# Layer 1's running means as products with banded matrices on TensorE, and router logits and expert rows summed in PSUM

## The chip, the cores and the metric

The kernel runs on one core of one Trainium2 chip. The metric is the device time of one execution in microseconds (us), the median of several runs. Beside it stands one profiled execution, with its own time and with a trace of every engine: TensorE (PE, with its weight loads as PEld), VectorE (DVE), ScalarE (ACT), GpSimd (POOL), and SyncE (SP), which issues most DMAs.

## The reference, cut to what matters

The program runs three blocks in a row on 256 tokens of width 1024 (and 16 meta tokens ahead of them in the first block). The change concerns the first block's layer 1: a pool of running means over the last 2, 4, 8 and 16 tokens for four groups of 256 columns, and the router of the experts behind it.

```python
def multiscale_pool(h, w_group, scale):
    hg = h.reshape(B, L, N_POOL_GROUPS, POOL_GROUP).astype(jnp.float32)
    pos = jnp.arange(L)
    for gi, w in enumerate(POOL_WINDOWS):            # (2, 4, 8, 16)
        xg = hg[:, :, gi, :]
        cs = jnp.cumsum(xg, axis=1)
        cs_shift = jnp.pad(cs, ((0, 0), (w, 0), (0, 0)))[:, :L]
        count = jnp.minimum(pos + 1, w).astype(jnp.float32)[None, :, None]
        outs.append((cs - cs_shift) / count - xg)
    pooled = jnp.stack(outs, axis=2).astype(h.dtype)
    mixed = jnp.einsum("blgc,gcd->blgd", pooled, w_group)
    return mixed.reshape(B, L, D_MODEL) * scale

def moe_swiglu(h, w_router, e_gate, e_up, e_down):
    logits = (h @ w_router).astype(jnp.float32)
    top_vals, top_idx = lax.top_k(logits, TOP_K)     # 2 of 8 experts
...
# layer 0: h += conformer_conv(rms_norm(h));  h += swiglu(rms_norm(h))
# layer 1: h += multiscale_pool(rms_norm(h)); h += moe_swiglu(rms_norm(h))
```

## The kernel before

**Stages.** Layer 0 (conformer convolution and a dense feed-forward), the pool and the router of layer 1, the experts of layer 1, then the second and the third block. All engines work from one program; each engine takes its instructions in a fixed order, and semaphores order them between engines. Weights stream from HBM in tiles of up to 1 MB; each is split by ACT (`whi`, L143) and DVE (`wlo`, L144) into a high and a low half, and each product of weights becomes three (`mm3`, L149 to L151).

**End of layer 0.** In `first_dense` the feed-forward's down projection runs over t = 0 to 3, two column tiles of 128 columns each. A t is 132 products of 128x272 into `pd` (22 tiles of the hidden width, three products, two column tiles). Then DVE adds `pd` to the residual `xT`, which lies column by token (L466), ACT squares it, ACT and DVE split it with the norm's gain (`xh`, `xl`), and 12 products with the pool's group weights (`pwh`, `pwl`) give two tiles of `mixed`, which ACT scales on its way out of PSUM (L480). The products of a t stand in PE's order among the first `pd` products of the next t; those of t = 3 stand behind the last `pd` product.

**Pool.** The group product is linear, so it stands ahead of the running means, and 1/rms (`r`) is needed only behind it. After t = 3, PE sums the squares (`ss`, L223), ACT and DVE form `r` (L227, L228), DVE and POOL multiply `mixed` by it (`z`, L647), POOL subtracts `z` from `xT` (L650), and DVE forms the running sums by scans along the tokens (L656, L659) and adds them to `xT` (L662). PE has 34 products without use in its order meanwhile (`K.heat`, L243, `HEAT1`).

**Router.** PE forms the logits experts by tokens (L700), and turns `xT` into rows token by column (L705), which ACT copies out twice (`xhi`, `row`) and from which POOL forms `xlo` (L708). The logits are turned (`LT`, L716 and L719), and `choose` takes the two best experts of each token by a chain of small DVE operations, up to the one-hot sum `M` (L755). PE forms slot numbers and counts from `M` (L757 to L764), with eight more idle products ahead of them (`HEAT2`), and DVE sorts the experts by load (`order`, L785).

**Experts.** PE gathers the rows of each expert by products with a selection matrix (L841), ACT and DVE split them (`gh`, `gl`), and the experts' products follow. SP loads the first 12 expert tiles ahead of the router's result; further tiles wait on SP for `order`, and for the buffers.

Of the kernel before, what the change touches and what calls it, by code (L numbers as in the profile page):

```python
# [8 lines left out]
F32 = mybir.dt.float32  # L9
# [22 lines left out]
HEAT0, HEAT1, HEAT2 = 10, 34, 8  # L32


def f(x):
    return x.bitcast(F32)
# [321 lines left out]
def first_dense(K, I, xT, r1, mixed):  # L358

# [6 lines left out]
    with ExitStack() as s0:  # L366
# [44 lines left out]
        with tc.tile_pool(name="ffn0", bufs=1, reuse_waits="tile") as fp:  # L411
# [39 lines left out]
            ss = K.tp_tile([P, T0], name="ss3")  # L451
            pw = [K.raw_tile([P, KC, 256], name=f"pw{n}", dt=F32R) for n in "hl"]
            K.split(*pw, K.load(I["pool_w_group"][0].rearrange("g (k p) n -> p (g k) n", p=P)))
            for t in range(4):
# [9 lines left out]
                for j in range(2):  # L464
                    c = 2 * t + j
                    nc.vector.tensor_add(xT[:, c, :], pd[j], xT[:, c, :])  # L466
                    K.add_square(fp, ss, xT[:, c, :], c, acc=acc)
                    if c == 0:
                        K.warm(AF.Sqrt, xT[:, c, :], square=True)
                xh, xl = (fp.tile([P, 2, T0], F32R, name=f"x{n}", bufs=2) for n in "hl")  # L470
                for j in range(2):
                    K.gain_split(xh[:, j, :], xl[:, j, :], xT[:, 2 * t + j, :], "mix1", 2 * t + j)
                for j in range(2):
# [6 lines left out]
                    nc.scalar.activation(mixed[:, c, :], ps, AF.Copy, scale=K.v("pool_scale", c))  # L480
            K.rstd(fp, r1, ss)
# [155 lines left out]
def first_pool(K, xT, mixed, r):  # L637

    tc, nc = K.tc, K.nc
    with tc.tile_pool(name="pool", bufs=1, reuse_waits="tile") as pp:
        z = pp.tile([P, KC, NMETA + T0], F32, name="z")
        nc.gpsimd.memset(z[:, :, 0:NMETA], 0.0)
        for g in (0, 1, 3, 2):
            cs = slice(2 * g, 2 * g + 2)
            (nc.gpsimd if g == 3 else nc.vector).tensor_mul(z[:, cs, NMETA:], mixed[:, cs, :],  # L647
                                                            r[:, None, :].to_broadcast([P, 2, T0]))
            if g:
                nc.gpsimd.tensor_sub(xT[:, cs, NMETA:], xT[:, cs, NMETA:], z[:, cs, 2 * NMETA:])  # L650
        for g in range(4):
            cs, w = slice(2 * g, 2 * g + 2), 2 << g
            win = pp.tile([P, 2, T0], F32, name="win", bufs=2)
            if g == 0:

                nc.vector.tensor_sub(win, z[:, cs, NMETA - 1:NMETA + T0 - 1], z[:, cs, NMETA:])  # L656
            else:
                for j in range(2):
                    nc.vector.tensor_tensor_scan(win[:, j, :], z[:, 2 * g + j, NMETA:],  # L659
                                                 z[:, 2 * g + j, NMETA - w:NMETA + T0 - w], 0.0,  # L660
                                                 op0=OP.add, op1=OP.subtract)
            nc.vector.scalar_tensor_tensor(xT[:, cs, NMETA:], win[:, :, NMETA:], 1.0 / w, xT[:, cs, NMETA:],  # L662
                                           op0=OP.mult, op1=OP.add)
# [5 lines left out]
class Moe:  # L669


    def __init__(self, K, I, pool, h3T, row, wr, i8, slots):
# [20 lines left out]
        with ExitStack() as s:  # L693
            tmp = s.enter_context(tc.tile_pool(name="route", bufs=1, reuse_waits="tile"))
            K.heat(K.onesr[:, None, :].to_broadcast([P, 4, P]), HEAT1)
            pl = K.mm_tile([NE, SEQ])

            def logits(c0, c1):
                for c in range(c0, c1):
                    nc.tensor.matmul(pl, wr[:, c, :], h3T[:, c, :], start=c == 0, stop=c == KC - 1)  # L700

            def turned(h, i, ps):
                ns = slice(h * 512, (h + 1) * 512)
                for q in range(4):
                    nc.tensor.transpose(ps[:, q * P:(q + 1) * P], h3T[:, 4 * h + q, i * P:(i + 1) * P], K.ident)  # L705
                nc.scalar.copy(self.xhi[:, i, ns], ps)
                nc.scalar.copy(row[:, i, ns], ps)
                nc.gpsimd.tensor_sub(self.xlo[:, i, ns], row[:, i, ns], f(self.xhi[:, i, ns]))  # L708

            logits(0, 4)  # L710
            turned(0, 0, K.tp_tile([P, 512]))
            logits(4, 6)
            turned(0, 1, K.tp_tile([P, 512]))
            logits(6, 8)
            LT = tmp.tile([NE, SEQ], F32, name="LT")
            nc.vector.tensor_copy(LT, pl)  # L716
            L = K.mm_tile([P, 2, NE])
            for i in range(2):
                nc.tensor.transpose(L[:, i, :], LT[:, i * P:(i + 1) * P], K.ident[0:NE, 0:NE])  # L719
            for i in range(2):  # L720
                turned(1, i, K.acc_tile([P, 512]))
            K.heat(self.xhi[:, 1, 0:512], HEAT2)
            self.choose(tmp, L, i8)
# [6 lines left out]
    def choose(self, tmp, L, i8):  # L730
# [31 lines left out]
        pc = K.tp_tile([P, NE])  # L762
# [283 lines left out]
def router_weights(K, I, pool):  # L1046

    nc = K.nc
    wr = pool.tile([P, KC, NE], F32, name="wr")
# [3 lines left out]
    i8 = pool.tile([P, 2, NE], F32, name="i8")  # L1053
# [5 lines left out]
def first_moe(K, I, h3T, row, router, routed, ahead, cap=P):  # L1059
    tc, nc = K.tc, K.nc  # L1060
    with ExitStack() as s0:
        pool = s0.enter_context(tc.tile_pool(name="moe", bufs=1, reuse_waits="tile"))
        K.more, K.bufs["more"] = s0.enter_context(tc.tile_pool(name="more", bufs=1, reuse_waits="tile")), 2
        moe = Moe(K, I, pool, h3T, row, *router, K.slots)
# [775 lines left out]
def body(tc, I, out):  # L1840
    nc = tc.nc
    with ExitStack() as ctx:
# [4 lines left out]
        r1 = cp.tile([P, T0], F32, name="r1")  # L1847
        mixed = cp.tile([P, KC, T0], F32, name="mixed")
        first_dense(K, I, xT, r1, mixed)
        cp = cols.enter_context(tc.tile_pool(name="cols2", bufs=1, side="right", reuse_waits="tile"))  # L1850
        router = router_weights(K, I, cp)
        first_pool(K, xT, mixed, r1)
# [44 lines left out]
```

## Time and profile before

| | |
|---|---|
| median of 3 runs | 2075.14 us (2074.33 to 2076.29) |
| profiled execution, own time | 2078.04 us |
| its span, first to last instruction | 2076.3 us (1.74 us of the time lie around it) |
| mean granted TensorE clock | 0.979 |
| PE busy | 1969.0 us, 95% of the span |
| DVE, ACT, POOL busy | 1598.0, 1252.4, 45.6 us |
| HBM read, mean rate | 502.39 MB, 243 GB/s |

The times of the trace are counted from the span's start. The last `pd` product of layer 0 begins at 370.82 us, and the first gather of expert rows at 401.03 us.

### The profile page before, as it was taken

What the parts mean: (1) busy time and instruction counts of PE and PEld (TensorE: products, weight loads), DVE (VectorE), ACT (ScalarE), POOL (GpSimd) and SP (SyncE); (2) the same over time, 40 slices, a digit from 0 to 9 for tenths busy, and PEclk for the clock granted to TensorE, in tenths of its full rate; (3) what the DMA queues carried; (4) which work ended last, traced back from release to release, by engine and by line L of the source; (5) the groups of instructions that cost most, each with busy time, mean ns of one, the idle gap of its engine ahead of it and who ended that gap; (6) DMA issues with size and microseconds to landing.
All of it is one profiled execution on the core that took longest, in us unless ns stands there. A gap on an engine that the chain in (4) does not pass through costs nothing. (4 is left out here: it accounts for less than half of the span.)

```text
span 2076.3 us, 29433 instructions
## 1 busy us (share of the span) xinstructions
PE 1969.0 (95%) x11342; PEld 1690.3 (81%) x11342; DVE 1598.0 (77%) x1949; ACT 1252.4 (60%) x1479; POOL 45.6 (2%) x74
## 2 busy tenths in 40 slices
PE   8999999899898998889988999998999999999998
PEld 7989999678676876668766778777889978989997
DVE  6967665788898988888888888887667677676664
ACT  6555444467786777766777677675356455645443
POOL 1100000200000000000000000001000010000000
PEclk8999999999999999999999999999999999999999
DMA  7115564589998999989999899985334553545552
GB/s 229 62 42 184 182 206 160 204 314 359 343 403 307 355 363 345 388 290 363 353 338 390 300 347 361 347 305 139 105 106 135 183 158 120 171 164 174 184 187 77
DMA packets 236269, 505.44 MB, mean 243 GB/s; under 512 B 12058, under 2 KB 130974, under 8 KB 236120
## 3 DMA queue, kind: packets, MB, share of 16 engines
q1 hardware_dynamic: 229268, 499.36, 68.6%
q10 hardware_dynamic: 5652, 2.35, 0.6%
q0 software_dynamic: 1200, 1.77, 0.3%
q8 instruction: 91, 1.49, 0.3%
q14 instruction: 58, 0.48, 0.1%
HBM read 502.39 MB, written 1.05 MB: 242 GB/s over the span
## 5 line engine op out<-in xcount | busy, mean ns | idle before, releaser
L144 DVE TENSOR_TENSOR wlo<-raw,whi 128x2048 fp32r<-128x2048 f32 (+3 forms) x618 | 1084.4, 1776 | 203.5 <-issue 72.6
L143 ACT CAST whi<-raw 128x2048 fp32r<-128x2048 f32 (+3 forms) x618 | 913.0, 1497 | 407.0 <-PE mm L150 138.7
L149 PE MATMUL mm<-uhi,whi 128*128 128x256 f32 (+2 forms) x1152 | 331.0, 290 | 4.5 <-ACT whi L143 2.5
L150 PE MATMUL mm<-ulo,whi 128*128 128x256 f32 (+2 forms) x1152 | 331.1, 288 | 0.0
L151 PE MATMUL mm<-uhi,wlo 128*128 128x256 f32 (+2 forms) x1152 | 330.0, 287 | 0.4 <-DVE wlo L138 0.4
L150 PE MATMUL mm<-wlo,gh 128*128 128x512 f32 x560 | 223.6, 399 | 5.4 <-DVE wlo L144 5.3
L149 PEld LDWEIGHTS mm<-uhi,whi 128*128 128x128 f32 (+1 forms) x1152 | 220.4, 193 | 8.9 <-ACT uhi L249 3.1
L149 PE MATMUL mm<-whi,gh 128*128 128x512 f32 x560 | 215.0, 402 | 9.6 <-ACT whi L143 6.8
L151 PEld LDWEIGHTS mm<-uhi,wlo 128*128 128x128 f32 (+1 forms) x1152 | 220.5, 192 | 2.8 <-issue 1.0
L151 PE MATMUL mm<-whi,gl 128*128 128x512 f32 x560 | 222.5, 397 | 0.0
L150 PEld LDWEIGHTS mm<-ulo,whi 128*128 128x128 f32 (+1 forms) x1152 | 221.1, 192 | 1.3 <-issue 0.7
L910 PE MATMUL mm<-wlo,gh 128*128 128x512 f32 x336 | 129.8, 421 | 34.9 <-DVE wlo L144 33.6
L149 PEld LDWEIGHTS mm<-whi,gh 128*128 128x128 f32 x560 | 106.1, 190 | 34.9 <-ACT whi L143 7.2
L150 PEld LDWEIGHTS mm<-wlo,gh 128*128 128x128 f32 x560 | 105.8, 189 | 34.8 <-DVE wlo L144 10.1
L909 PE MATMUL mm<-whi,gh 128*128 128x512 f32 x336 | 123.1, 402 | 2.7 <-ACT whi L143 2.7
L151 PEld LDWEIGHTS mm<-whi,gl 128*128 128x128 f32 x560 | 105.7, 189 | 24.5
L910 PEld LDWEIGHTS mm<-wlo,gh 128*128 128x128 f32 x336 | 59.5, 191 | 67.6 <-DVE wlo L144 58.2
L150 PE MATMUL py<-wlo,mhh 128*128 128x512 f32 x280 | 112.3, 401 | 0.0
L151 PE MATMUL py<-whi,mhl 128*128 128x512 f32 x280 | 110.8, 396 | 0.0
L150 PE MATMUL mm<-vlo,whi 128*128 128x272 f32 x352 | 102.4, 291 | 0.0
L151 PE MATMUL mm<-vhi,wlo 128*128 128x272 f32 x352 | 101.7, 289 | 0.0
L149 PE MATMUL py<-whi,mhh 128*128 128x512 f32 x280 | 101.6, 396 | 0.0
(646 smaller groups left out, 3159.6 us busy)
## 6 DMA issues: line engine op xcount, KB each, us to landing
raw<-in_moe_w_gate_dram SPq DMA_DIRECT2D x112, 1024.0 KB, 7.0
raw<-in_moe_w_up_dram SPq DMA_DIRECT2D x112, 1024.0 KB, 6.7
raw<-in_moe_w_down_dram SPq DMA_DIRECT2D x112, 1024.0 KB, 7.1
raw<-in_w_in_dram SPq DMA_DIRECT2D x40, 1024.0 KB, 5.2
raw<-in_w_ffn_in_dram SPq DMA_DIRECT2D x22, 1024.0 KB, 5.1
raw<-in_conv_w_pw_dram SPq DMA_DIRECT2D x12, 1024.0 KB, 10.2
raw<-in_ffn_w_gate_dram SPq DMA_DIRECT2D x11, 1024.0 KB, 5.4
raw<-in_ffn_w_up_dram SPq DMA_DIRECT2D x11, 1024.0 KB, 5.4
```

The costliest lines, as they stand in the source:

```text
L143: nc.scalar.copy(hi[:, ks, :], raw[:, ks, :])
L144: nc.vector.tensor_sub(lo[:, ks, :], raw[:, ks, :], f(hi[:, ks, :]))
L149: mm(out, lhi, rhi, start=start, stop=False)
L150: mm(out, lhi, rlo, start=False, stop=False)
L151: mm(out, llo, rhi, start=False, stop=stop)
L909: nc.tensor.matmul(out, hi, whi, start=start, stop=False)
L910: nc.tensor.matmul(out, hi, wlo, start=False, stop=stop)
```

## The change

A class `Mix` takes the place of `first_pool`. It needs no scan: with tokens on the partitions, a running mean over w tokens is a product with a banded 128x128 matrix, `diag` (1/w within the band, and -1 on the diagonal), plus a small product with `over` for the tokens ahead of the 128. The matrices are built by DVE from an iota (`start`), and their rows are scaled by 1/rms of each token (`factors`), so that `mixed` itself is not multiplied.

- Each tile of `mixed` is turned as it arrives (`turn`): three transposes and three small products with the router's weights, into one PSUM tile `mixt`, from which DVE and ACT copy rows (`mixr`) and partial logits (`mixl`).
- The sum of squares is formed token by token in one column (`sst`, six products of one column).
- The rows that the experts need are summed in four PSUM tiles `row`: `xT` turned by products with the identity (`own_rows`), the banded products (`window_rows`), and a product with zeros that closes the sum (`close`). Logits are summed token by expert in `L`, in the same way.
- ACT forms `xhi` and `row` from PSUM, DVE forms `xlo` from PSUM; POOL's part is gone. `HEAT1` is gone, `HEAT2` is 16 in place of 8.

```diff
-HEAT0, HEAT1, HEAT2 = 10, 34, 8
+HEAT0, HEAT2 = 10, 16
...
                 for j in range(2):
                     c = 2 * t + j
                     nc.vector.tensor_add(xT[:, c, :], pd[j], xT[:, c, :])
-                    K.add_square(fp, ss, xT[:, c, :], c, acc=acc)
+                    sq = acc if c == 0 else fp.tile([P, T0], F32, tag="sq", name="sq", bufs=2)
+                    nc.scalar.activation(sq, xT[:, c, :], AF.Square)
+                    if 0 < c < KC - 1:
+                        nc.vector.tensor_add(acc, acc, sq)
...
+                if t == 3:
+                    mix.factors(acc, sq)
...
-                    nc.scalar.activation(mixed[:, c, :], ps, AF.Copy, scale=K.v("pool_scale", c))
-            K.rstd(fp, r1, ss)
+                    mixed = fp.tile([P, T0], F32, name="mixed", bufs=2)
+                    nc.scalar.activation(mixed, ps, AF.Copy, scale=K.v("pool_scale", c))
+                    mix.turn(c, mixed)
...
-def first_pool(K, xT, mixed, r):
...
-        for g in (0, 1, 3, 2):
-            cs = slice(2 * g, 2 * g + 2)
-            (nc.gpsimd if g == 3 else nc.vector).tensor_mul(z[:, cs, NMETA:], mixed[:, cs, :],
-                                                            r[:, None, :].to_broadcast([P, 2, T0]))
-            if g:
-                nc.gpsimd.tensor_sub(xT[:, cs, NMETA:], xT[:, cs, NMETA:], z[:, cs, 2 * NMETA:])
...
+class Mix:
...
+    def factors(self, *squares):
...
+        for i, at in enumerate((NMETA, NMETA + P, 0)):
+            for n, sq in enumerate(squares):
+                nc.tensor.matmul(ss[:, i:i + 1], sq[:, at:at + P], K.mean_w[:, 0:1], start=n == 0, stop=n == 1)
+        nc.scalar.activation(r, ss[:, 0:3], AF.Sqrt, bias=K.eps[:, 0:1])
+        nc.vector.reciprocal(r, r)
+        nc.vector.tensor_scalar(self.diag[1], self.diag[0], r[:, 1:2], None, op0=OP.mult)
...
+    def turn(self, c, mixed):
...
+        ps = K.tp_tile([P, 4, P], name="mixt")
+        for i, (at, n) in enumerate(((NMETA, P), (NMETA + P, P), (0, NMETA))):
+            nc.tensor.transpose(ps[0:n, i, :], mixed[:, at:at + n], K.ident)
+            nc.tensor.matmul(ps[0:n, 3, i * NE:(i + 1) * NE], mixed[:, at:at + n], self.wr[:, c, :],
+                             start=True, stop=True)
...
+    def window(self, ps, i, g, of):
...
+        mm(ps, self.diag[i][:, g, :], of(i), start=False, stop=False)
+        if i:
+            mm(ps[0:NMETA], self.over[0][:, g, :], of(0), start=False, stop=False)
+        else:
+            mm(ps[0:NMETA], self.over[1][0:NMETA, g, :], of(2), start=False, stop=False)
...
-            K.heat(K.onesr[:, None, :].to_broadcast([P, 4, P]), HEAT1)
...
-                nc.gpsimd.tensor_sub(self.xlo[:, i, ns], row[:, i, ns], f(self.xhi[:, i, ns]))
...
+            own_rows(0)
             for i in range(2):
+                for c in range(KC):
+                    nc.tensor.matmul(L[:, i, :], own(i, c), mix.wr[:, c, :], start=i == c == 0, stop=False)
+            own_rows(1)
+            window_rows(0)
+            split_rows(0)
             for i in range(2):
+                for g in range(4):
+                    mix.window(L[:, i, :], i, g,
+                               lambda t: mix.logits[0:NMETA if t == 2 else P, g, t, :])
+            mix.close(L.rearrange("p i e -> p (i e)"))
+            window_rows(1)
+            self.choose(tmp, L, mix.i8)
+            split_rows(1)
```

How the order of instructions moves is seen at three places. The first is PE at the start of t = 1 of the down projection (the same at t = 2 and 3), where the pool products of t = 0 (into `mm`) end and the `pd` products of t = 1 go on; before:

```order
L150 MATMUL mm<-xl,pwh 128x272
L151 MATMUL mm<-xh,pwl 128x272
L149 MATMUL pd_3240<-hhi,whi 128x272
L150 MATMUL pd_3240<-hlo,whi 128x272
L151 MATMUL pd_3240<-hhi,wlo 128x272
```

And now, at the same place:

```order
L151 MATMUL mm<-xh,pwl 128x272
L149 MATMUL pd_3308<-hhi,whi 128x272
L150 MATMUL pd_3308<-hlo,whi 128x272
L151 MATMUL pd_3308<-hhi,wlo 128x272
L696 MATMUL mixt<-ident,mixed 128x128
L697 MATMUL mixt<-wr,mixed 128x8
L696 MATMUL mixt<-ident,mixed 128x128
L697 MATMUL mixt<-wr,mixed 128x8
L696 MATMUL mixt<-ident,mixed 16x128
L697 MATMUL mixt<-wr,mixed 16x8
```

Three `pd` products later the first of two column tiles is turned; the same six rows follow once more for the second, and then `pd` goes on. The second place is PE from the sum of squares behind the last `pd` product to the first gather; before (the products with `mixed`'s weights stand between the first rows, and are left out):

```order
L243 MATMUL heat<-onesr,identr 128x512 x28
L700 MATMUL mm<-xT,wr 8x256 x4
L705 MATMUL tp<-ident,xT 128x128 x4
L700 MATMUL mm<-xT,wr 8x256 x2
...
L719 MATMUL mm<-ident,LT 128x8 x2
L705 MATMUL acc<-ident,xT 128x128 x3
L243 MATMUL heat<-xhi,identr 128x512 x8
L757 MATMUL mm<-M,upper 128x16
L758 MATMUL mm<-M,onesr 128x8
L764 MATMUL tp<-M,onesr 128x8 x2
L841 MATMUL tp<-sel,xhi 128x256
```

And now (left out: the two turns of t = 3 behind the first L714, the other rows of the four sums, and the like rows of the logits' sum):

```order
L766 MATMUL row_4003<-ident,xT 128x128 x3
L786 MATMUL mm<-wr,xT 128x8 x16
L150 MATMUL mm<-xl,pwh 128x272
...
L714 MATMUL row_4003<-mixr_97,diag_101 128x256
...
L714 MATMUL mm<-mixl,diag_100 128x8
L718 MATMUL mm<-mixl,over_103 16x8
...
L724 MATMUL row_4005<-onesr,zero 128x512
L835 MATMUL mm<-M,upper 128x16
L836 MATMUL mm<-M,onesr 128x8
L842 MATMUL mm<-M,onesr 128x8 x2
L243 MATMUL heat<-xhi,identr 128x512 x16
L919 MATMUL tp<-sel,xhi 128x256
```

The 28 idle products are gone, sixteen 8-column products (L786) stand before the last pool products, and the idle products of the end stand behind those with `M`. The third place is DVE between the reciprocal and `M`; before, the reciprocal is followed by:

```order
L228 RECIPROCAL r_94<-r_94 128x272
L647 TENSOR_TENSOR z<-mixed,r_94 128x2x272 x3
L656 TENSOR_TENSOR win<-z 128x544
L659 SCALAR_TENSOR_TENSOR win<-z 128x272
L662 SCALAR_TENSOR_TENSOR xT<-win,xT 128x2x256
```

And now DVE's rows from the logits to `M` hold two splits of rows, and a third right ahead of `M`:

```order
L781 TENSOR_TENSOR xlo<-row_4002,xhi 128x512
L822 TENSOR_REDUCE m<-mm 128x2
L824 TENSOR_TENSOR t<-mm,m 128x16
L781 TENSOR_TENSOR xlo<-row_4003,xhi 128x512
L825 SCALAR_TENSOR_TENSOR t<-t,i_95 128x16
...
L827 TENSOR_TENSOR oh_4082<-i_95,ix 128x16
L781 TENSOR_TENSOR xlo<-row_4004,xhi 128x512
L833 TENSOR_TENSOR M<-oh_4081,oh_4082 128x16
```

The scans are gone from DVE, and the splits that POOL did stand among the choice. The building of the matrices (21 rows) stands at the very start of DVE's order, ahead of the first copy L196. SP's order of DMAs is the same as before, and from the gather on so are the orders of PE, ACT and DVE.

## Rows read from the trace of the kernel before

**Rows 1.** The page, busy time of each engine (share of the span, instructions):

```profile
PE 1969.0 (95%) x11342; PEld 1690.3 (81%) x11342; DVE 1598.0 (77%) x1949; ACT 1252.4 (60%) x1479; POOL 45.6 (2%) x74
```

**Rows 2.** Busy time by stretch, within the down projection (columns in the first line):

```profile
core 0: us, PE busy (x) PEld busy (x) DVE busy (x) ACT busy (x) POOL busy (x), PEclk, DMA share, GB/s
300.00:365.00 65.00, 64.96 (x514) 64.38 (x514) 33.34 (x43) 29.09 (x44) 0.00 (x0) 1.00 0.59 192
```

**Rows 3.** Timeline (start, duration, engine, line; in brackets idle time before), pool and router:

```profile
370.95 0.62 PE L223 MATMUL ss<-acc,mean_w 128*128 128x272 f32 x2
...
372.78 0.72 PE L223 MATMUL ss<-sq,mean_w 128*128 128x272 f32 x2 [0.23 <-ACT sq L216]
...
376.45 4.27 DVE L647 TENSOR_TENSOR z<-mixed,r 128x544 f32<-128x544 f32 x3
...
384.84 3.56 PE L700 MATMUL mm<-xT,wr 128*8 128x256 f32 x8 [3.02 <-issue]
...
392.45 0.17 DVE L744 TENSOR_REDUCE m<-mm 128x2 f32<-128x16 f32 x1 [0.50 <-PE mm L719]
...
397.18 0.17 DVE L755 TENSOR_TENSOR M<-oh,oh 128x16 fp32r<-128x16 f32 x1
...
401.03 0.55 PE L841 MATMUL tp<-sel,xhi 128*128 128x256 f32 x1 [2.96 <-DVE slotr L801]
...
402.95 0.42 ACT L249 ACTIVATE gh<-tp,vec 128x192 fp32r<-128x192 f32 x1 [6.52 <-PE tp L841]
```

**Rows 4.** Timeline, PE: products with few columns, wide ones, transposes, idle products:

```profile
1720.29 0.36 PE L1692 MATMUL sc<-ml_sp,ones 128*128 128x4 f32 x2
1720.51 0.36 PE L1693 MATMUL sc<-ml_sp,upto 128*128 128x4 f32 x2
...
1758.74 0.59 PE L1661 MATMUL acc<-Z,sv 128*128 128x256 f32 x2
1759.17 0.39 PE L1662 MATMUL acc<-Z,sv 128*128 128x128 f32 x2
1759.39 0.38 PE L1661 MATMUL acc<-Z,sv 128*128 128x256 f32 x1
...
389.88 0.66 PE L705 MATMUL tp<-ident,xT 128*128 128x128 f32 x4
391.43 0.77 PE L705 MATMUL acc<-ident,xT 128*128 128x128 f32 x5
375.27 6.55 PE L243 MATMUL heat<-onesr,identr 128*128 128x512 f32 x28
```

**Rows 5.** Timeline, DVE and POOL within the choice, and a DVE operation of 128x512:

```profile
392.72 3.77 POOL L708 TENSOR_TENSOR xlo<-row,xhi 128x512 fp32r<-128x512 f32 x3 [0.44 <-ACT row L707]
392.87 1.18 DVE L747 SCALAR_TENSOR_TENSOR t<-t,i 128x16 f32<-128x16 f32 x1
394.29 1.01 DVE L749 TENSOR_TENSOR oh<-i,ix 128x16 f32<-128x16 f32 x1
396.56 0.17 DVE L747 SCALAR_TENSOR_TENSOR t<-t,i 128x16 f32<-128x16 f32 x1
387.75 0.66 DVE L662 SCALAR_TENSOR_TENSOR xT<-win,xT 128x512 f32<-128x512 f32 x1
```

**Rows 6.** Busy time by stretch, columns as in rows 2: the granted clock:

```profile
385.00:388.00 3.00, 3.00 (x8) 0.64 (x6) 3.00 (x6) 0.00 (x0) 0.00 (x0) 0.50 1.03 411
388.30:392.60 4.30, 4.30 (x26) 2.38 (x26) 2.21 (x8) 2.71 (x7) 1.89 (x2) 1.00 0.37 129
401.00:405.20 4.20, 4.17 (x18) 4.10 (x19) 2.00 (x9) 1.64 (x4) 0.00 (x0) 0.50 0.01 4
647.60:651.00 3.40, 1.97 (x16) 1.86 (x16) 3.40 (x7) 0.60 (x2) 0.00 (x0) 1.00 0.99 377
651.00:657.80 6.80, 5.18 (x12) 4.09 (x13) 1.16 (x3) 2.76 (x3) 0.00 (x0) 0.50 0.68 258
```

**Rows 7.** Timeline, DVE's first copy at the program's start:

```profile
6.90 0.17 DVE L196 COPY vec<-tp 128x16 f32<-128x16 f32 x1 [5.07 <-PE tp L195]
```

**Rows 8.** Timeline, SP: last of the twelve early expert loads, and the next:

```profile
375.34 1.40 SPq L118 DMA_DIRECT2D raw<-in_moe_w_gate_dram  x3
404.55 0.37 SPq L118 DMA_DIRECT2D raw<-in_moe_w_up_dram  x1
```

More of the change, by code (lines that the diff above doesn't have):

```diff
@@ L710, in __init__ @@
[L710 to L717, printed above, removed]
-            for i in range(2):
-                nc.tensor.transpose(L[:, i, :], LT[:, i * P:(i + 1) * P], K.ident[0:NE, 0:NE])
-            for i in range(2):
-                turned(1, i, K.acc_tile([P, 512]))
+            L = K.mm_tile([P, 2, NE])
@@ new lines, in __init__, with own, own_rows @@
+            rows = [[(K.tp_tile if h else K.acc_tile)([P, 512], name=f"row{h}{i}") for i in range(2)]
+                    for h in range(2)]
+            def own(i, c):
+                return xT[:, c, NMETA + i * P:NMETA + (i + 1) * P]
+            def own_rows(h):
+                for i in range(2):
+                    for q in range(4):
+                        nc.tensor.matmul(rows[h][i][:, q * P:(q + 1) * P], own(i, 4 * h + q), K.ident,
+                                         start=q == 0, stop=False)
@@ new lines, in window_rows, with split_rows @@
+            def window_rows(h):
+                for i in range(2):
+                    for g in (2 * h, 2 * h + 1):
+                        gs = slice(g * 256, (g + 1) * 256)
+                        mix.window(rows[h][i][:, g % 2 * 256:(g % 2 + 1) * 256], i, g,
+                                   lambda t: mix.rows[t][:, gs])
+                    mix.close(rows[h][i])
+            def split_rows(h):
+                ns = slice(h * 512, (h + 1) * 512)
+                for i in range(2):
+                    nc.scalar.copy(self.xhi[:, i, ns], rows[h][i])
+                    nc.vector.tensor_sub(self.xlo[:, i, ns], rows[h][i], f(self.xhi[:, i, ns]))
@@ L722, in __init__ @@
+            window_rows(1)
+            self.choose(tmp, L, mix.i8)
+            split_rows(1)
+            for h in range(2):
+                for i in range(2):
+                    nc.scalar.copy(row[:, i, h * 512:(h + 1) * 512], rows[h][i])
             K.heat(self.xhi[:, 1, 0:512], HEAT2)
-            self.choose(tmp, L, i8)
             for i in range(2):
@@ L1056, in router_weights, with first_moe @@
     return wr, i8
-def first_moe(K, I, h3T, row, router, routed, ahead, cap=P):
+def first_moe(K, I, xT, row, mix, routed, ahead):
     tc, nc = K.tc, K.nc
@@ L1860, in ahead @@
                 K.pre[f"b2{k}"] = K.load(parts)
-        first_moe(K, I, xT[:, :, NMETA:], row, router, cols.close, ahead)
+        first_moe(K, I, xT, row, mix, cols.close, ahead)
         second_block(K, I, row, rows)
```

90 lines of the change are left out of this document (53 added, 37 removed).

## The prediction

> **What bounds the kernel now.** I read the busy times of the engines first: PE has 95% of the span, DVE 77%, POOL 2% [rows 1]. So PE is the bound nearly everywhere, and what counts is where the change puts work on a full PE, and where PE stood waiting. Next the stretches by busy time. In the down projection of layer 0 PE works 64.96 of 65.00 us at full clock, while the DMAs are busy 0.59 of the time [rows 2]: each product added there lengthens the program by its own duration. Last the timeline behind that stage [rows 3]. From the first sum of squares (370.95) to the first gather of expert rows (401.03) lie 30.1 us in which PE does little that the result needs: DVE multiplies (376.45, three times), scans, and lets PE form logits from 384.84 on; the choice begins at 392.45, `M` stands at 397.18, the gather follows at 401.03 and the first split of gathered rows at 402.95. This tail is bounded by DVE's chain, not by PE. The change therefore moves work from a chain on DVE to a PE that is free in the tail and full before it.
>
> **Added to the down projection.** The turns of t = 0, 1 and 2 stand among `pd` products of the next t. A turn of one column tile is three transposes and three products of 8 columns in fp32. A transpose costs 0.11 us, the difference between five (0.77) and four (0.66) [rows 4]. For the product of 8 columns the nearest rows are the products of 4 columns with a 128x128 fp32 stationary matrix, which begin 0.22 us apart (1720.29, 1720.51) [rows 4]; the bounds are 0.11, if one weight load is all that is paid, and 0.22. Five at 0.22, and 0.33 for the transposes, less the small ones of the 16 tokens, give 0.88 a turn with 0.22, and about 0.6 with 0.11. Six turns: **+5.3 us** (from 3.6 to 5.3; 0 only if PE weren't the bound, against rows 2). I take the upper end, since the row with few columns is the nearer. DVE and ACT get twelve small copies a t, and have half of the stage free (33.34 and 29.09 of 65 busy, rows 2).
>
> **The tail, step by step, at full clock.** I count from the first sum of squares, 370.95 in the trace [rows 3].
> - The last square reaches PE at +1.8 (372.78), as before [rows 3]; six pool products, three of the turned tiles and the first of six `sst` products fit ahead of it.
> - Then five `sst` products (0.22 each, as above), five 128x128 products of `own_rows` (0.22: 1759.17 to 1759.39 [rows 4]), two pool products of 272 columns (0.126: 65 us by 514 [rows 2]), sixteen logit products L786 (16 by 0.22 = 3.5), four pool products and one banded product of 256 columns (0.43: 1758.74 to 1759.17 [rows 4]): 1.1 + 1.1 + 0.25 + 3.5 + 0.5 + 0.43 = 6.9, so +8.7.
> - Two turns, 1.76: +10.4. Seven banded products by 0.43, eight of `own_rows` by 0.22, two closing products of 512 columns by 0.23 (a heat product: 6.55 by 28 [rows 4]): 5.2, so +15.7.
> - Eight logit windows at 0.22, eight with a 16-column stationary matrix at about half of that: 2.7. Logits at +18.4; before at 392.45, or +21.5.
> - The choice took 4.73 from 392.45 to 397.18 [rows 3]. In it two operations lasted 1.18 and 1.01 while POOL formed `xlo` for 3.77; the first of these took 0.17 in the second round [rows 5]. With a third one like them (0.78 in place of 0.17) that is 2.4 which goes with POOL's work. In come two splits of 128x512 on DVE, at 0.6 each by the 0.66 of such an operation [rows 5]. So 3.5, and `M` at +21.9 against +26.2.
> - `M` to gather took 3.85 (397.18 to 401.03) and gets one more split: +26.4. The sixteen idle products behind `M`'s own (16 by 0.234 = 3.7 [rows 4]) just fit below it. Before: +30.1. **-3.7 us.**
> - The gather ran at half clock (401.00 to 405.20 at 0.50 [rows 6]), 1.92 from its first product to the first split. Behind sixteen idle products at full clock it would need half: **-0.9 us.**
>
> Building the matrices costs nothing: DVE is idle 5.07 us ahead of its first copy [rows 7], and 21 operations of at most 0.3 us fill most of that, but not more; without that cover it would be 4 us. SP's loads cost nothing either: twelve tiles are ahead at 375.34, and the next load at 404.55 comes 3.5 us behind the gather [rows 8], so it waits for a buffer and not for the order of experts; it moves with the gather.
>
> **The clock, which I charge.** In the trace the clock falls to half behind stretches in which PE does little: after 16 small products within 3.40 us (1.97 busy, 647.60 to 651.00) it was 0.50 for 6.80 us [rows 6]. It doesn't come back with the first full work: 385.00 to 388.00 and 401.00 to 405.20 are full of products and still at 0.50, and full clock stands in the row behind the first of them [rows 6]. The sixteen L786 products take 3.5 us with 8 columns each, which is less than those 16 products do. Behind them stand 0.5 of pool products, 0.43, and 1.76 of turns, again mostly 8 columns and short transposes, and only then 5.2 us of wide products. So I expect half clock from about the end of L786 through the turns (2.7 us more), then over a stretch of wide products like the two rows that are full and at 0.50 (3.0 and 4.2 us long, half of which is loss: 1.5 to 2.1 more), and in a little of L786 itself (0.5): **+5.0 us**, with the bounds 0 (no fall) and 8 (half clock through the logit windows, 2.7 more).
>
> The Trainium skill, TensorE: Matmul & The Clock Gate, Part 4, says that a transpose in PE's transpose mode doesn't count as busy PE for the clock. The stretch with eleven transposes stayed at 1.00 (388.30 to 392.60 [rows 6]), but it holds products of 256 columns too, so the trace neither bears the rule out nor excludes it.
>
> **Sum.** 5.3 - 3.7 - 0.9 + 5.0 = +5.7 us. The trace is of an execution of 2078.04 us (span 2076.3, and 1.74 around it), 2.9 above the median of the runs; so about 2083.7 for a like execution, and **2080.8 us** against the median of 2075.14.
>
> **Rivals.**
> - *The clock holds, or falls for one short stretch.* Then the clock costs 0 to 2, and if the 8-column products cost less than 0.22 the turns are cheaper too: 2075.8 to 2078, no change that can be told. For it: 388.30 to 392.60 stayed at 1.00 with 26 short products [rows 6]. Against: those products had up to 256 columns. It decides if L786 ends at full clock.
> - *The clock stays down through the logit windows.* Their small products (2.7 us) keep it down, and the second half of the rows runs at half clock: +8 in place of +5.0, so 2083.8; with the idle products at half clock too (7.4 in place of 3.7, against 4.45 free) up to 2086.
> - *The turns are hidden.* If the end of the down projection were set by the split of its weights, six turns would cost nothing: 2075.8 - 5.3 = 2070.5, faster. It decides if PE shows idle time there; 64.96 of 65.00 busy [rows 2] speaks against it.
> - *Turns lower the clock in the down projection.* Three times a turn pair between wide products; if each cost a stretch of 3.4 us at half clock, that is 3 by 1.7 = 5.1 more: 2086. Against it: each pair is only 1.8 us long, with full work on both sides. The Trainium skill's rule on transposes, named above, would favour this one.
>
> **How the numbers follow.** The forecast has 0.42 (its own range 2079 to 2082.5), the clock that holds 0.27, the clock that stays down longer 0.18, the hidden turns 0.08, the falls in the down projection 0.05. From 2074.5 to 2085 lie all but the hidden turns, half of the falls, and the worst of the third. A measurement tells 0.2% of this kernel, 4.15 us, from no change: below 2071.0 is faster, above 2079.3 slower. Faster is the hidden turns, 0.08; within the bound lie the clock that holds and a sixth of the forecast (its lower edge, 0.07), 0.34; the rest, 0.58, is slower.
>
> **What the profile would show.** The step on the turns is right if six groups of L696 and L697 take 0.9 us each between `pd` products and PE has no idle time there; wrong if L697 begins less than 0.2 us after its transpose. The tail is right if the choice begins 18 to 24 us behind the last `pd` product and lasts 3.5 us with no operation of 128x16 over 0.3 us. The clock's step is right if L714 and the turns stand in a stretch at 0.50; a clock of 1.00 from the end of the down projection to the gather makes the prediction wrong by 5. A DVE that delays L196 past 6.90, or an `sst` chain that holds up the banded products, would make it wrong at places where I charge nothing.

## The result and the profile after

The changed kernel takes **2093.42 us** (median of 5 runs, 2087.62 to 2099.67) against 2075.14 before: ratio 1.0084, 95% interval 1.0071 to 1.0096. It is slower, as forecast, but by 18.3 us in place of 5.7, and outside the range of 2074.5 to 2085.0. The profiled execution took 2087.62 us, 9.6 more than that of before. Of the five runs it is the fastest, and its start is 4.4 us ahead of the trace of before: the clock was at half from 8.6 to 18.8 us, there until 26.4. With that taken out, the traces differ by 14.0. (The start is measured at the first `pd` product: 295.10 us against 299.45.)

The page answers to [rows 1]. PE works 19.8 us more, and GpSimd 12.5 less:

```profile
PE 1988.8 (95%) x11495; PEld 1704.7 (82%) x11495; DVE 1592.3 (76%) x2003; ACT 1254.5 (60%) x1487; POOL 33.1 (2%) x65
```

The timeline of PE at the third of the three joints of the down projection shows one pair of turns, where before stood nothing (start, duration, engine, line, operation):

```profile
355.99 0.29 PE L151 MATMUL pd<-hhi,wlo 128*128 128x272 f32 x1
356.28 0.33 PE L696 MATMUL mixt<-ident,mixed 128*128 128x128 f32 x1
356.44 0.29 PE L697 MATMUL mixt<-wr,mixed 128*128 128x8 f32 x2
356.59 0.30 PE L696 MATMUL mixt<-ident,mixed 128*128 128x128 f32 x1
...
358.00 0.21 PE L697 MATMUL mixt<-wr,mixed 128*16 128x8 f32 x2
358.14 0.39 PE L149 MATMUL pd<-hhi,whi 128*128 128x272 f32 x1
```

From 355.99 to 358.14 lie 2.15 us, of which a `pd` product alone would take 0.13. From the first `pd` product to the last it is 77.7 us in place of 71.4: the three joints cost 6.3. No gap stands in them, and the clock stays at 1.00.

Behind the down projection the busy time by stretch, in the columns of [rows 2], answers to [rows 6]:

```profile
377.20:380.60 3.40, 3.40 (x34) 3.40 (x32) 0.54 (x2) 0.00 (x0) 0.00 (x0) 1.00 1.02 411
380.70:391.00 10.30, 10.30 (x43) 7.82 (x44) 1.69 (x13) 1.47 (x4) 0.00 (x0) 0.51 1.01 399
391.10:397.60 6.50, 6.50 (x41) 4.01 (x39) 0.69 (x1) 2.38 (x5) 0.00 (x0) 1.00 0.04 14
397.70:401.10 3.40, 3.40 (x12) 1.81 (x13) 2.03 (x11) 0.59 (x1) 0.00 (x0) 0.50 0.00 0
401.20:408.00 6.80, 6.80 (x14) 1.90 (x13) 1.29 (x5) 1.17 (x2) 0.00 (x0) 0.51 0.00 0
408.10:411.00 2.90, 2.90 (x14) 2.27 (x15) 2.10 (x12) 2.50 (x7) 0.00 (x0) 1.00 0.00 0
```

PE is never idle here. The clock falls at 380.7, behind the sixteen L786 products, and again at 397.7, at the end of the thin logit windows ("thin" stands for products of 8 columns); 20.5 us run at half clock. What that costs is read below, from a run in which the same products run at full clock.

The timeline of DVE and PE from the logits to the gather answers to the last rows of [rows 3]:

```profile
398.87 0.17 DVE L822 TENSOR_REDUCE m<-mm 128x2 f32<-128x16 f32 x1 [4.98 <-PE mm L724]
401.40 0.17 DVE L827 TENSOR_TENSOR oh<-i,ix 128x16 f32<-128x16 f32 x1
404.43 0.69 DVE L781 TENSOR_TENSOR xlo<-row,xhi 128x512 fp32r<-128x512 f32 x1 [2.85 <-ACT xhi L780]
405.04 0.17 DVE L833 TENSOR_TENSOR M<-oh,oh 128x16 fp32r<-128x16 f32 x1
398.76 1.22 PE L714 MATMUL row<-mixr,diag 128*128 128x256 f32 x2
406.98 1.03 PE L716 MATMUL row<-mixr,over 128*16 128x256 f32 x2
408.36 0.28 PE L835 MATMUL mm<-M,upper 128*128 128x16 f32 x1
412.65 0.28 PE L919 MATMUL tp<-sel,xhi 128*128 128x256 f32 x1
```

The choice has its second expert at 401.40, but `M` stands behind a split in DVE's order, which waits for rows that PE forms at half clock; and `M`'s products stand on PE behind all of the second half's windows, which run from 398.76 to 408.36. From the last `pd` product (372.78) to the gather this **tail** takes 39.9 us, against 30.2 before (370.82 to 401.03).

### The profile page after: what moved, and what is told of

It reads as the page before. It is cut to its first block, busy times and chain, and to the rows that moved or that the text cites. A ratio compares the mean times of both kernels' runs of the same rounds, so it can differ in the third digit from the quotient of the medians.

```text
span 2085.8 us, 29795 instructions
## 1 busy us (share of the span) xinstructions
PE 1988.8 (95%) x11495; PEld 1704.7 (82%) x11495; DVE 1592.3 (76%) x2003; ACT 1254.5 (60%) x1487; POOL 33.1 (2%) x65
```

## The experiments

In each, the tail is taken from the trace of one execution, as above; times are medians against the kernel before in the same job.

**a_again: the changed kernel once more.**

> The changed kernel once more, for a second trace. Clock theory: the excess over the forecast is TensorE at half clock in the tail behind the down projection, 380.7 to 391.0 and 397.7 to 408.0 in the first trace; the second trace again shows two such stretches there, about 20 us in sum, and the runs spread over 8 us or more, since the place of the stretches moves from run to run. Rival, more work on TensorE: the tail is long because of the added products, and the runs' spread comes from elsewhere, the start of the program above all, where the first trace was 4.4 us ahead of the trace of before: then the tail stays at 39.9 us within 1 us and the difference lies in the first 30 us. Median 2093 by both.

2092.38 us (2087.64 to 2103.31, six runs) against 2076.91, ratio 1.0082 (1.0060 to 1.0104). The second trace (2091.18 us) has the long start, half clock until 25.8, and the same tail, 39.9 us, with half clock in the same places, counted from the last `pd` product (376.40). By stretch:

```profile
376.50:384.10 7.60, 7.60 (x70) 7.60 (x68) 4.38 (x9) 2.99 (x5) 0.00 (x0) 1.00 1.00 395
384.30:394.30 10.00, 10.00 (x40) 7.53 (x41) 1.69 (x13) 1.48 (x4) 0.00 (x0) 0.50 1.02 401
```

So the start explains the distance of the two traces, 3.6 us, and the rival is right on that; it doesn't tell why the tail is long.

**n_noturn: no turns at t = 0 to 2** (the pool's part of these columns is left out).

```diff
-                    mix.turn(c, mixed)
+                    if t == 3:
+                        mix.turn(c, mixed)
```

> The changed kernel without the turns of the first six column tiles (t = 0 to 2; the pool's part of these columns is left out, their rows and logits are zeros). Theory: the three steps of 2.1 us between the products of the down projection go, all of them, since TensorE is full there; the tail behind it stays as it is, 39.9 us with two half-clock stretches: 6.3 us less, median 2085 to 2088. Rival, that the turns are part hidden, or that their thin products cost in other places too: under 3 us or over 9 us less.

2089.54 us (2078.67 to 2093.71) against 2075.00, ratio 1.0059 (1.0038 to 1.0080): above the expected range. In the trace all 6.3 us are gone: from the first `pd` product (299.18) to the last (370.51) it is 71.3 us, as in the kernel before. But the tail, with the same products as the changed kernel's, took 44.7 us, not 39.9, since half clock began earlier and lasted longer:

```profile
377.30:390.70 13.40, 13.40 (x56) 10.88 (x56) 1.69 (x13) 1.48 (x4) 0.00 (x0) 0.50 0.89 344
390.90:397.60 6.70, 6.70 (x44) 4.23 (x43) 0.69 (x1) 2.38 (x5) 0.00 (x0) 1.00 0.02 7
397.80:414.60 16.80, 16.80 (x37) 8.70 (x38) 7.22 (x42) 4.88 (x11) 0.00 (x0) 0.50 0.00 0
```

So the step on the turns holds by the trace; the medians, 14.5 us over the kernel before in place of 15.5 and 18.3, don't show 6.3, and the tail did not stay as it was, against the expectation. The same tail can cost 5 us more in another execution.

**c_few: 14 of the 16 logit products L786 left out** (so the experts chosen are others, and what follows the gather may differ too).

```diff
-                for c in range(KC):
+                for c in range(1):
                     nc.tensor.matmul(L[:, i, :], own(i, c), mix.wr[:, c, :], start=i == c == 0, stop=False)
```

> Leaves out 14 of the 16 logit products of the residual (L786), so the choice of experts is another one. Clock theory: 14 by 0.22, 3.1 us of work, goes, and with it the first half-clock stretch (10.3 us, of which 5.1 are loss): tail 31 to 33 us, median 2085. Rival, the work itself: 3.1 us less, tail 36.8 us, median 2090.

2084.71 us (2083.60 to 2090.36), ratio 1.0044 (1.0027 to 1.0062); tail 32.4 us. As the clock theory said, the first half-clock stretch is gone: 7.5 us less tail for 3.1 us less work, so that the stretch had cost 4.4 us, less than half of its 10.3. Full clock lasts nearly to the end of the logit windows, and there it falls, as in the changed kernel:

```profile
379.50:389.00 9.50, 9.50 (x57) 5.85 (x56) 2.61 (x16) 2.57 (x6) 0.00 (x0) 1.00 1.02 409
389.00:392.20 3.20, 3.20 (x29) 2.84 (x28) 0.00 (x0) 1.21 (x3) 0.00 (x0) 1.00 1.03 411
392.40:402.50 10.10, 10.10 (x23) 3.65 (x23) 3.39 (x16) 1.75 (x3) 0.00 (x0) 0.50 0.08 31
```

This trace also gives the price of the products at full clock. The timeline of PE:

```profile
386.92 0.60 PE L716 MATMUL row<-mixr,over 128*16 128x256 f32 x2
387.46 0.70 PE L714 MATMUL row<-mixr,diag 128*128 128x256 f32 x2
388.09 0.60 PE L716 MATMUL row<-mixr,over 128*16 128x256 f32 x2
388.62 0.49 PE L724 MATMUL row<-onesr,zero 1*128 1x512 f32 x1
389.04 0.39 PE L714 MATMUL mm<-mixl,diag 128*128 128x8 f32 x2
389.36 0.20 PE L718 MATMUL mm<-mixl,over 16*16 16x8 f32 x2
389.49 0.39 PE L714 MATMUL mm<-mixl,diag 128*128 128x8 f32 x2
```

From start to start, a window product of 256 columns takes 0.53 to 0.63 here, where [rows 4] gave 0.43, a closing product 0.42, where I had 0.23, and a pair of thin ones 0.45, where I had 0.33. Counted from the first sum of squares, as in the prediction, the logits stand at +18.4 us, the last 0.8 of them at half clock; with the 3.1 of work that was left out, at +21.4, and not at +18.4; before it was +21.5.

These prices also give the cost of the second stretch of half clock in the changed kernel, as an estimate. The second half's four pairs of windows (1.17 each, 386.92 to 388.09) and two closing products would take 5.5 us at full clock; they took 9.6 (398.76 to 408.36), 4.1 more, and the last thin windows lost some 0.4. Both stretches together cost about 8.9 us of 20.5.

**b_mixed and w_wide: the order of thin and wide products.** b_mixed has the same products, each L786 emitted behind a product of `own_rows`, each logit window behind a row window. w_wide also takes the residual's logits in the form of before:

```diff
-                for c in range(KC):
-                    nc.tensor.matmul(L[:, i, :], own(i, c), mix.wr[:, c, :], start=i == c == 0, stop=False)
...
+            for c in range(KC):
+                nc.tensor.matmul(pl, mix.wr[:, c, :], xT[:, c, NMETA:], start=c == 0, stop=c == KC - 1)
+            nc.vector.tensor_copy(LT, pl)
+            for i in range(2):
+                nc.tensor.matmul(L[:, i, :], LT[:, i * P:(i + 1) * P], K.ident[0:NE, 0:NE],
+                                 start=i == 0, stop=False)
```

> The same products in another order: each 8-column logit product is emitted behind a 128-column product of the turned rows, each logit window behind a 256-column window of the rows. No product is added or left out. Clock theory: shorter runs of thin products, so less half clock; the tail from the last product of the down projection to the first gather falls from 39.9 to 30 to 36 us, the median to 2081 to 2088. Rival, the work itself: the tail stays at 39 to 41 us, the median at 2091 to 2095.

> The residual's logits in the form of before (eight products of 256 columns, then turned by two small products into the same sum), and each logit window behind a 256-column window of the rows. TensorE's work in the tail is the same within 1 us. Clock theory: full clock up to the choice, tail 29 to 32 us, median 2079 to 2083, runs within 4 us of each other. Rival, the work itself: tail 39 to 41 us, median 2091 to 2095, spread of 8 us or more.

b_mixed took 2094.08 us (2086.41 to 2099.05), ratio 1.0084 (1.0065 to 1.0103); in its trace (2088.26 us) the clock held up to 401.7, and the tail was 36.1 us, as the clock theory said, but its median was not; the traced execution is 5.8 us under it. w_wide was a plain miss: 2095.64 us (2091.32 to 2097.29), ratio 1.0086 (1.0073 to 1.0100), tail 45.6 us. The L786 stretch was gone, and yet the clock fell at 393.8 and stayed at half to the gather. By stretch:

```profile
387.00:390.30 3.30, 3.30 (x27) 3.03 (x26) 0.00 (x0) 0.00 (x0) 0.00 (x0) 1.00 1.01 410
390.40:393.70 3.30, 3.30 (x18) 1.69 (x18) 0.00 (x0) 0.00 (x0) 0.00 (x0) 1.00 1.02 408
393.90:409.00 15.10, 15.10 (x46) 6.88 (x44) 0.00 (x0) 0.00 (x0) 0.00 (x0) 0.50 0.22 86
```

PE has no idle time ahead of the fall. What stands in 390.40 to 393.70 are row windows L714 (128 rows) and L718 (16 rows, those of the meta tokens), each 256 columns wide and nearly equally long, with thin pairs between. That gave a new theory: products that read 16 rows don't hold the clock up, however many columns they move.

**q_full: w_wide with 128 rows in L718, of which 112 are zeros** (in the row windows and in the logit windows).

```diff
-            mm(ps[0:NMETA], self.over[1][0:NMETA, g, :], of(2), start=False, stop=False)
+            mm(ps[0:NMETA], self.over[1][:, g, :], of(2), start=False, stop=False)
```

> w_wide with one difference: the products with the 16 meta tokens (L718) read 128 rows, of which 112 are zeros, in place of 16. Same number of products, same columns, same durations. In w_wide the clock fell at 393.8, in a stretch in which TensorE had no idle time but half of the 256-column products had 16 rows. Theory that products with 16 rows don't hold the clock up: full clock up to the choice, tail 32 to 36 us against 45.6, median 2081 to 2087. Rival, that only the 8-column products bring it down: the clock falls as in w_wide, tail 43 to 47 us, median 2093 to 2097.

2090.30 us (2085.13 to 2091.11), ratio 1.0071 (1.0057 to 1.0085); tail 37.6 us in place of 45.6. Tail and median lie between the ranges of theory and rival, in neither. The clock did as the theory said: it held through all windows and fell at 402.1, where PE waits for `M`; the sixteen idle products then ran at half clock ahead of the gather:

```profile
387.20:400.00 12.80, 12.80 (x66) 6.39 (x64) 0.00 (x0) 0.00 (x0) 0.00 (x0) 1.00 0.57 228
400.10:402.00 1.90, 1.24 (x6) 0.71 (x5) 1.40 (x6) 1.32 (x3) 0.00 (x0) 1.00 0.00 0
402.20:408.80 6.60, 3.69 (x11) 3.11 (x12) 5.60 (x34) 4.92 (x14) 0.00 (x0) 0.50 0.00 0
```

In w_wide the windows of the last 128 tokens, all of 128 rows, ran at half clock from 397.9 to 409.1 without bringing it back; here the same windows ran at 1.00.

**k_rows and k_cols: the mechanism by itself.** In the kernel before, where PE waits anyway, the 34 idle products of `HEAT1` read 16 rows (k_rows), or have 16 columns of weights (k_cols). For k_rows:

```diff
-            K.heat(K.onesr[:, None, :].to_broadcast([P, 4, P]), HEAT1)
...
+                nc.tensor.matmul(hp, K.identr[0:NMETA, :], K.onesr[0:NMETA, None, :].to_broadcast([NMETA, 4, P]),
+                                 start=True, stop=True)
```

> The kernel before with its 34 idle products (HEAT1) of 128 rows, 128 columns of weights and 512 moving columns replaced by 34 products of 16 rows, otherwise alike: same time on TensorE each, 0.23 us. Theory that products with 16 rows don't hold the clock up: TensorE has no idle time from 375.3 to 381.8, as before, and yet the clock falls to 0.50 within that stretch, 3 us or more ahead of its fall at 384.8 in the trace of before. Rival, only the columns count: full clock up to the end of the idle products.

> The kernel before with its 34 idle products replaced by 34 of 128 rows and 16 columns of weights (16 output rows), otherwise alike. Theory: it is the rows read that count; the clock stays at 1.00 through the idle products, and falls where it did before, about 3 us behind their end. Rival, the share of the array in use counts: it falls as in k_rows.

One execution each: 2078.04 and 2075.49 us, beside 2075.05. In k_rows the clock fell at 374.4, within the idle products, which all ran on without a gap, and stayed at half to 388.1:

```profile
373.10:374.30 1.20, 1.20 (x6) 0.96 (x7) 1.10 (x2) 0.63 (x2) 0.49 (x1) 1.00 1.01 396
374.50:384.00 9.50, 9.50 (x23) 6.91 (x21) 9.50 (x9) 0.00 (x0) 6.21 (x4) 0.50 1.03 414
```

In k_cols one stretch of 28 of these products took 6.65 us at full clock, and the clock fell at 382.2, behind their end, as in the kernel before:

```profile
372.83 6.65 PE L697 MATMUL heat<-onesr,identr 128*16 128x512 f32 x28
```

In these two traces, one of each, it is the rows that count and not the columns of weights; the tail of k_rows is 31.7 us, 1.5 longer.

**v_heat: idle products in the changed kernel**, eight among L786 and eight among the logit windows:

```diff
+                    if c % 2:
+                        K.heat(K.onesr[:, None, :].to_broadcast([P, 4, P]), 1, K.sc_tile([P, 512]))
...
+                    K.heat(mix_hot, 1, K.sc_tile([P, 512]))
```

> The changed kernel with sixteen idle products of 512 columns more (16 by 0.23, 3.7 us of added work on TensorE), eight among the logit products L786 and eight among the logit windows. Clock theory: no half clock, or a short one, from the down projection to the choice; 10.2 us of loss go and 3.7 come: tail 31 to 35 us against 39.9, median 2083 to 2088, and runs closer together than the 16 us of the changed kernel. Rival, the work itself: 3.7 us more, tail 43.5 us, median 2096.

2091.82 us (2089.13 to 2096.31), ratio 1.0080 (1.0063 to 1.0097); tail 39.4 us, so neither was right; the median is 4 us above the clock theory's range. The first fall was avoided, the second came at 399.2. It cost most by the queue: `M` was formed at 402.57, but its products began only at 409.75, behind the windows at half clock:

```profile
407.17 1.22 PE L714 MATMUL row<-mixr,diag 128*128 128x256 f32 x2
408.32 1.03 PE L716 MATMUL row<-mixr,over 128*16 128x256 f32 x2
409.29 0.54 PE L724 MATMUL row<-onesr,zero 1*128 1x512 f32 x1
409.75 0.28 PE L839 MATMUL mm<-M,upper 128*128 128x16 f32 x1
```

**z_best and z_hot: the idea as well as I could order it.** Both are q_full with the choice emitted ahead of the second half's windows (below), and the logit windows among those of the first half; z_hot has eight idle products among the logit windows besides, and six in place of sixteen at the end.

```diff
-            window_rows(1)
...
             self.choose(tmp, L, mix.i8)
...
+            window_rows(1)
```

> q_full with two changes of order: the logit windows stand among the windows of the first half of the rows, and the choice is emitted ahead of the windows of the second half, so that TensorE forms those during the choice and the products with M no longer stand behind all of them. Theory (half clock, and the queue ahead of M's products): full clock from the down projection to the gather, logits at +22 to +23 us, gather at +29 to +31 us; what stays is the three turns, 6.3 us, and the median is 2079 to 2082, slower than before by 3 to 6. Rival, that something outside this tail costs: the tail shortens as said, and the median stays above 2086.

> z_best with eight idle products of 512 columns among the thin logit windows (1.9 us of added work), and six in place of sixteen behind M's products. In z_best the clock fell at 398.6, behind a stretch of windows of which half the time went to thin products, and the sixteen idle products ran at half clock ahead of the gather. Theory that half clock is what is left of the tail's loss: full clock up to the gather, logits at +24 us, gather at +30.5 to +32.5 us, median 2079 to 2083 and runs closer together. Rival, the work itself: gather at +39 to +41 us, median 2086 or more.

z_best: 2085.82 us (2081.78 to 2090.81), ratio 1.0041 (1.0026 to 1.0055). Its logits came at +22.2 as expected, but in the traced execution the clock fell at 398.6, and the gather came at +38.4. Its median lies 4 us above the theory's range and just under the rival's 2086. z_hot: 2085.96 us (2081.12 to 2089.41), ratio 1.0047 (1.0034 to 1.0060). Its clock did what the theory said, full to the gather, and its tail was 33.3 us, 0.8 over the range:

```profile
374.30:398.00 23.70, 23.70 (x153) 16.15 (x151) 6.52 (x23) 4.38 (x9) 0.00 (x0) 1.00 0.89 352
398.00:407.40 9.40, 8.59 (x31) 4.01 (x30) 7.34 (x39) 6.60 (x15) 0.00 (x0) 1.00 0.00 1
```

Even so it is 3.1 us longer than the tail of before, and with the turns' 6.3 that makes 9.4, where the medians differ by 11.0. The median was 3 us over the expected range and just under the rival's, so that full clock alone does not bring the time back.

**e_split and h_only: two parts of the change alone, in the kernel before.** e_split forms `xlo` on DVE from PSUM; h_only has 20 idle products ahead of `M`'s and 14 behind them, so that the gather runs at full clock. g_heat is both, with 14 ahead and 14 behind.

```diff
-                nc.gpsimd.tensor_sub(self.xlo[:, i, ns], row[:, i, ns], f(self.xhi[:, i, ns]))
+                nc.vector.tensor_sub(self.xlo[:, i, ns], ps, f(self.xhi[:, i, ns]))
```

> The kernel before with one part of the change alone: xlo is formed by VectorE from PSUM in place of GpSimd from SBUF. Theory of the prediction: GpSimd's reads stretched three operations of the choice by 2.4 us in sum; they take 0.2 each now, VectorE gets four splits of 0.65, two of them ahead of M, so the choice takes 3.5 us in place of 4.73 and the gather comes 0.5 to 1.5 us earlier: median 2073.5 to 2076. Rival: all four splits stand ahead of the choice's end on VectorE, and the gather comes 0.2 to 1 us later, median 2077 to 2078.

> The kernel before with idle products alone changed: twenty in place of eight ahead of M's products, fourteen behind them, so that TensorE is busy up to the gather. Theory: the tail keeps its 30.2 us, the gather and the first products run at full clock in place of 0.50 (401.00 to 405.20 in the trace of before), as in the changed kernel, whose time from gather to end is 2.0 us shorter: median 2073 to 2074.5. Rival: the gather's half clock lies beside the expert's weights, or the idle products hold M's products up; then 2075 to 2077.

> e_split with idle products up to the gather, fourteen ahead of M's products and fourteen behind. Theory: the two add up, 0.5 us of tail and 2.0 behind the gather: median 2072.5 to 2074, faster than before by 0.1%. Rival: as for h_only, 2075 to 2077.

e_split: 2075.42 us (eleven runs, 2073.83 to 2079.02), ratio 1.0000 (0.9991 to 1.0009). The two stretched operations of [rows 5] took 0.17 each, and from the logits' first reduction to `M` it took 3.4 us in place of 4.7:

```profile
389.15 0.16 DVE L744 TENSOR_REDUCE m<-mm 128x2 f32<-128x16 f32 x1
389.52 0.69 DVE L708 TENSOR_TENSOR xlo<-acc,xhi 128x512 fp32r<-128x512 f32 x1
390.13 0.17 DVE L747 SCALAR_TENSOR_TENSOR t<-t,i 128x16 f32<-128x16 f32 x1
392.54 0.17 DVE L755 TENSOR_TENSOR M<-oh,oh 128x16 fp32r<-128x16 f32 x1
```

But the logits came 0.8 later, and the tail was 29.7, 0.5 us less, which the medians don't tell from nothing. h_only: 2076.75 us (2071.46 to 2079.74) against 2077.44, ratio 0.9994 (0.9985 to 1.0003), though its clock was full all through the gather:

```profile
384.80:401.50 16.70, 16.70 (x98) 13.00 (x97) 12.46 (x58) 9.49 (x23) 5.70 (x5) 1.00 0.27 100
```

g_heat: 2078.32 us (2072.49 to 2079.84), ratio 1.0004 (0.9996 to 1.0013), where 2072.5 to 2074 was expected. No version tried is faster than the kernel before by more than the runs can tell.

## Why the prediction was wrong

The sign was right, and so was the bound: PE was full in the down projection, and the tail became PE's. The terms put at nothing held as well: DVE's first copy came at 6.57 us, before the 6.90 of before, and SP's next load 3.3 us behind the gather. The size failed, and two steps failed most: the tail at full clock (-3.7) and the clock (+5.0, for one stretch of half clock).

- **Turns, +5.3: measured +6.3.** Fully on the path (in n_noturn's trace all of it is gone). As the prediction words it, five products at 0.22 and 0.33 make 1.43 a turn; its 0.88 is what three products at 0.22 and the transposes give. A turn took 0.93: its thin products 0.14 to 0.15, less than the upper bound taken, its transposes 0.14 to 0.20 in place of 0.11. The rest, 0.26 a pair, lies at the change from `pd` products to turns and back, which I had not counted.
- **The tail at full clock, -3.7: about +0.8.** That is 39.9 less the 8.9 that half clock cost in it, against 30.2. Two things were wrong. I priced a window product at 0.43, as in a chain of [rows 4], a closing one at 0.23 and a thin pair at 0.33; with 0.53 to 0.63, 0.42 and 0.45 the logits come at about +21.4 in place of +18.4, hardly earlier than before (c_few). And I let `M`'s products follow `M`, 3.5 us behind the logits. They stand in PE's order behind the second half's windows, which take 5.5 us behind the logits even at full clock. The choice itself was priced fairly: POOL's stretch went (e_split).
- **The clock, +5.0: about +8.9.** I charged one stretch of half clock, from L786 "through the turns" and "then over a stretch of wide products", and that stretch came: 10.3 us, as the sum implies, and it cost 4.4. What the sum had at nothing is a second one. The logit windows are sixteen thin products as well, and the clock fell at their end; by the estimate above that cost another 4.5. My rival "the clock stays down through the logit windows" had the second half of the rows at half clock, with +8, but not the way to it: the clock was back at 1.00 from 391.1 to 397.6, through most of the logit windows. `M` to gather was 7.6 us where I had 4.5, since at half clock the second half's windows hold back the split ahead of `M` and then `M`'s products.
- **The gather at full clock, -0.9: open.** It ran at full clock, 0.9 us from its first product to the first split in place of 1.9. But h_only has the same, and its median is 0.7 lower with an interval from 3.1 lower to 0.6 higher, which excludes neither nothing nor 0.9. From gather to end the traces vary by more than that: 1672.3 us in q_full, 1673.2 in the changed kernel, 1675.3 before, 1678.2 in h_only and 1678.4 in z_hot.

What brought the clock down is shown in part. For the first stretch it is the L786 products: it is gone with 14 of the 16 left out (c_few) or with idle products among them (v_heat). It is not the 16-row windows, of which only one stands whole in it (386.55). That windows of 16 rows can bring the clock down, and that padding them keeps it up, is shown for the order of w_wide, and for idle products in the kernel before. No run pads the rows in the changed kernel's own order, so what 16 rows and what 8 columns do in its second stretch is not shown; eight idle products among the logit windows did not prevent it (v_heat).

Two smaller readings of the prediction are off without bearing on its sum: the row from 388.30 to 392.60 holds fifteen 128-column transposes, eleven of them up to 391.8, and the idle products at half clock would bring the second rival to 2086.8, not 2086.

The corrected terms, 6.3 + 0.8 + 8.9, give +16.0; but that is no more than the turns and the tail of one execution, and its nearness to the medians (+18.3 and +15.5 in two jobs) is in part luck. The traced execution itself took 2087.62 us, 12.5 over the median before. Set beside its own traced execution in the same way, turns and longer tail come near in c_few (8.5 against 8.0), b_mixed (12.2 against 11.4), w_wide (21.7 against 20.4), v_heat (15.5 against 16.0) and n_noturn (14.5 against 16.0), and miss by 3 to 4 us in the changed kernel's first trace, q_full (13.7 against 9.3), z_best (14.5 against 11.0) and z_hot (9.4 against 12.7).

The Trainium skill's rule on transposes (TensorE: Matmul & The Clock Gate, Part 4) favoured a rival to which I gave 0.05, and that rival did not come: the clock stayed at 1.00 through all three joints of the down projection. Each holds 1.9 us of turns between full work, so it says little on the rule itself.

What stays open is the spread. The changed kernel's runs lie 12 and 16 us apart in two jobs, those of before 2 to 6. The start gives up to 4.4 of it, and n_noturn shows that the same tail can have 30 us of half clock in place of 20. But half clock is not all of it. Every run has its mean granted clock, and over such a span a difference of 0.001 is worth at most some 2 us. The run of 2096.01 us has 0.974, against 0.978 in the traced one of 2087.62, which fits; but that of 2093.42 has 0.980, a higher clock than the traced one. Two runs of q_full at 0.983 lie 6 us above its traced one at 0.982. So some 5 us in several runs, and so in the medians, lie in something that no trace here caught. Nor do I know what moves the time from gather to end by 6 us.

## What to carry to other kernels

Work that is moved onto a waiting TensorE is free only at the price of its own form: before pricing it, look at how many rows and columns each product has, for in these traces a stretch of thin or few-row products was followed by half clock, and so the work behind it cost more too. Padding rows with zeros took no time in the product (0.53 a window either way, w_wide and q_full) and kept the clock up. And when a chain is shortened, look for what is queued ahead of its next step on each engine: here `M` was ready 3 to 7 us before TensorE came to it, and at full clock too the windows ahead of it would have taken longer than the choice.

## What the runs showed of the hardware

A TensorE without any idle time fell to half clock: 34 products of 512 columns with 16 rows each brought it down within the stretch (k_rows: 0.50 from 374.4), the same with 128 rows and 16 columns of weights did not (k_cols: 28 of them in 6.65 us at 1.00). Each was traced once. Half clock did not double the time of the work under it: the second half's windows took 9.6 us where c_few's prices give 5.5. The fp32 windows of 256 columns took 0.1 to 0.2 us more than the products of [rows 4] (0.53 to 0.63 against 0.43, all at full clock); no run shows why. Small DVE operations of 128x16 that took 1.18 and 1.01 us beside POOL's splits took 0.17 when DVE did the splits itself (e_split). And the half clock at the program's start ends at 18.8 us in one execution and at 25.8 in another of the same kernel, which moves all that follows by 3.6 us.
